# A kernel whose instruction order is written by its own estimate of times: the estimate learns a lock between two engines

## The chip, the cores and the metric

The kernel runs on one core of a Trainium2 chip. A core has TensorE (PE, matmuls into PSUM), VectorE (DVE), ScalarE (ACT), GpSimd (POOL) and SyncE (SP), which issues most of the transfers. Each engine works through its own list of instructions in order, and an instruction waits until the data that it reads are there. The metric is the time on the device in microseconds, the median of several runs.

## The reference

One inference step of a decoder layer on 1024 new prompt rows and 8 x 4 sample rows (1056 in all, width 1024, float32):

```
h = rmsnorm(x, norm_mix);  p = h @ w_in + b_in          # 1024 -> 4104
mLSTM heads (4): causal conv and silu on q, k; gates i, f; chunked scan with states C, n, m
HGRN2 heads (4): sigmoid gates f; chunked scan with state S
mix = concat(sigmoid(o) * headnorm(mLSTM), headnorm(HGRN2) * silu(g))
x = x + mix @ w_out
h2 = rmsnorm(x, norm_ffn)
x = x + (silu(h2 @ w_gate) * (h2 @ w_up)) @ w_down      # 1024 -> 2816 -> 1024
outputs: rmsnorm(x, norm_final) and the conv, C, n, m, S states of prompt and samples
```

## The kernel before, in words

Every dense product is made of three fast matmuls: an operand is rounded to a short format (the tiles HI for activations and whi for weights) and what the rounding left is kept beside it (LO and wlo); hi x hi, hi x lo and lo x hi are summed. ScalarE makes the rounded part and VectorE or GpSimd the rest, which the text calls the rest of a weight or of a row. `split(t, pool)` does this for weight tile t, 1024 columns in two chunks of 512 (L212 rounds, L213 makes the rest).

The 1056 rows lie in three blocks of 288, 384 and 384. The projection is a list of `units`, each one output tile of 128 columns for one block: 24 matmuls (L254, L256, L257; in the first unit of a block the low products come last, L265). For each of four mLSTM heads there are four weight tiles times three blocks, preceded by one tile for the gates (units 0, 6 and 11), and then the same for four HGRN2 heads. Unit 5 is block 1's first, unit 10 block 2's first. Then come the output projection `w_out` (units from `first_wo` on, by quarters of 264 rows), the second norm `norm2`, a few plain feed-forward tiles, and from some 700 us on the rest of the feed-forward in a scheme with fewer products, whose order is written out by step counts.

Everything beside the dense units is written as Python generators that emit instructions in pieces and are interleaved with the units: `startup(b)` (first norm of block b: sums of squares, a power on GpSimd, a transpose that spreads it over the partitions, then per row tile a scaling on VectorE L1940, a rounding on ScalarE L1943 and a rest L1947), `gates` and `gates_sample` (running sums and maxima for the mLSTM gates), `conv`, `mix_a` (mLSTM: L685 to L766), `mix_b` (HGRN2), `sample_core`, `split`, `mix_split` (rounds the mixers' output), `norm2`. Between matmuls `hook` steps them. A piece is emitted either after a count of hooks (`yield 2`) or when `need(e, ...)` says yes: the kernel keeps an estimate of each engine's time, of each tile's last write and read and of the transfers (`now`, `wrote`, `read`), advanced by `estimate()` with `cost()` for each instruction, and `need` asks whether the operands are there by that engine's time and whether that engine is at most 2.0 us ahead of TensorE. `finish(key)` forces a generator to its end where its result is needed next. So the numbers in `cost` decide the order of the instructions, and nothing else: the order is fixed when the program is built.

Weight tiles live in rings: two raw buffers, five whi and five wlo (`NRAW`, `NW`). In the kernel before, tiles 2 to 8 (`NAUTO = 9`) are rounded when `need("ACT", raw)` agrees, later ones by hook counts, and all the rests from tile 2 on are made by GpSimd. SP's list is in order: a load that waits for its buffer holds what is behind it.

Of the kernel before, what the change touches and what calls it, by code (L numbers as in the profile page):

```python
# [10 lines left out]
F32 = mybir.dt.float32  # L11
# [30 lines left out]
def hybrid_step(ctx: ExitStack, tc: tile.TileContext, i, o):  # L42
# [17 lines left out]

    now = dict(PE=0.0, DVE=0.0, ACT=0.0, POOL=0.0, SP=0.0, dma=0.0, n=0, tab="T", on=True)
    wrote, read, rings, pred, cap = {}, {}, {}, {}, {}
    ENG = {"PE": "PE", "DVE": "DVE", "Activation": "ACT", "Pool": "POOL", "SP": "SP"}

    def keys_of(ap):
# [17 lines left out]
    def all_keys(aps):  # L83
        return [k for a in aps if hasattr(a.tensor, "tag_meta") for k in keys_of(a)]

    def cost(e, op, x, n):
        if e == "PE":
            a = x.ins[0]
            if a.dtype == F32R:
                return 0.0076 + 0.000433 * n  # L90
            return 0.01 + n * (0.00078 if "transpose" in x.concise()[:400].lower() else 0.0017)
        if e == "DVE":
            return 0.13 + (0.0018 if "Scan" in op else 0.00104) * n
        if e == "ACT":
            c = 0.1 + 0.00083 * n
            f = str(getattr(x, "func", ""))
            for tab, fs in (("L", ("Ln",)), ("T", ("Tanh",)), ("S", ("Sigmoid", "Silu"))):
                if any(f.endswith(y) for y in fs) and now["tab"] != tab:
                    now["tab"] = tab
                    c += 1.28  # L100
            return c
        return 0.25 + 0.002 * n

    def estimate():
        if not now["on"]:
            return
        for x in islice(nc.all_instructions(), now["n"], None):
            now["n"] += 1
            e = ENG.get(str(x.engine).split(".")[-1])
            outs = [a.bass_ap for a in x.outs if hasattr(a, "bass_ap")]  # L110
            if e is None or not outs:
                continue
            ins = [a.bass_ap for a in x.ins if hasattr(a, "bass_ap")]
            op = str(x.opcode)
            n = 1
            for q in outs[0].ap[1:]:
                n *= q[1]
            ko, ki = all_keys(outs), all_keys(ins)
            t = max([now[e]] + [wrote.get(k, 0.0) + 0.06 for k in ki])
            for k in ko:  # L120
                if not (e == "PE" and k in wrote):
                    t = max(t, touched(k) + 0.06)
                if k not in wrote and pred[k[0]]:
                    t = max(t, read.get(pred[k[0]], 0.0) + 0.06)
            if "DMA" in op:
                now[e] = t + 0.4
                now["dma"] = max(now["dma"], t) + n * outs[0].ap[0][1] * 4 / 385e3
                end = now["dma"] + 1.8
            else:
                now[e] = t + cost(e, op, x, n)  # L130
# [8 lines left out]
    def need(e, *aps, banks=0, tags=(), lead=0.0):  # L139
        def ok():  # L140
            t = max([wrote.get(k, 0.0) for k in all_keys(aps)] + [0.0])
            for tag, m in (("mx", banks), *((x, 1) for x in tags)):
                for full in rings:
                    if m and full.startswith(tag + "_"):
                        r, b = rings[full], cap[full]
                        t = max([t] + [read.get(k, 0.0) for k in r[-b:][:m] if len(r) >= b])
            if e == "PE":
                return t <= now["PE"] + lead
            return t <= max(now["PE"], now[e]) + lead and now[e] <= now["PE"] + 2.0
        return ok  # L150

    def start(gen, key, wait=1):
        active.append([gen, key, wait])
# [34 lines left out]
                if callable(e[2]) and (e[1] == key or k > 8):  # L188
                    step_gen(e)

    NW, NRAW, NAUTO = 5, 2, 9
    raws, his, los = {}, {}, {}

    def load(t):
# [4 lines left out]
    def split(t, pool):  # L199
        while t not in raws or (t and t - 1 not in his):  # L200
            yield 1
        hi = his[t] = wp.tile([128, 1024], F32R, tag="whi", name="whi", bufs=NW)
        lo = los[t] = wp.tile([128, 1024], F32R, tag="wlo", name="wlo", bufs=NW)
        n, raw = tile_n[t], raws[t]
        auto = t >= 2 and t < NAUTO
        for c in range(0, n, 512):
            if auto:
                yield need("ACT", raw)
            elif c:
                yield 2  # L210
            s = slice(c, c + 512)
            nc.scalar.activation(hi[:, s], raw[:, s], AF.Copy)  # L212
            (nc.gpsimd if pool else nc.vector).tensor_tensor(lo[:, s], raw[:, s], hi[:, s].bitcast(F32), op=OP.subtract)  # L213
# [117 lines left out]
    nc.scalar.dma_start(vec, i["vec"])  # L331
    maskneg, seqm, mneg4 = cst[:, 0:128], cst[:, 128:136], cst[:, 136:168]
    mk = {0: msk[:, 80:112], **{l: msk[:, 16 * j:16 * j + 16] for j, l in enumerate(LEVELS)}}
    nc.scalar.preload_act_table_set("sqrt_and_others")
    ones = cn.tile([128, 1], F32, name="ones")
    nc.vector.memset(ones, 1.0)
    mhalf = cn.tile([128, 5], F32, name="mhalf")
# [2 lines left out]
    def col(j):  # L340
        return vec[:, j:j + 1]

    def ntile(tag="nt"):
        if tag in ("raw", "W"):
            return mp.tile([128, 387], F32, tag=tag, name=tag, bufs=2 if tag == "raw" else 1)
        if tag == "na":
            return cn.tile([128, QN], F32, tag=tag, name=tag, bufs=1)
        return cn.tile([128, 384], F32, tag=tag, name=tag, bufs=2)

    def norm_rstd(key, n, acc, w=(2, 3)):  # L350

# [89 lines left out]
    def gates(ps, b):  # L441
# [16 lines left out]
        nc.scalar.activation(a, f, AF.Abs)  # L458
        nc.scalar.activation(a, a, AF.Exp, scale=-1.0)
        nc.scalar.activation(a, a, AF.Ln, bias=1.0)  # L460
        yield need("DVE", a)
        nc.vector.scalar_tensor_tensor(lf, f, 0.0, a, op0=OP.min, op1=OP.subtract)
        nc.vector.tensor_copy(me[:, 0:1], mcar)
# [40 lines left out]
    def gates_sample(ig, lf):  # L504
# [19 lines left out]
        g, em, wl, ng, wi = (r[:, j] for j in range(5))  # L524
        nc.vector.tensor_tensor(g, s4(ig), F4, op=OP.subtract)
        nc.vector.tensor_tensor(ng, F4, m4, op=OP.subtract)
        nc.scalar.activation(em, m4, AF.Exp, scale=-2.0)
        nc.vector.tensor_tensor(wi, ng, m0s[:, :, None].to_broadcast([4, 8, 4]), op=OP.add)
        nc.scalar.activation(wi, wi, AF.Exp)
        nc.vector.tensor_tensor(wl, g, ng[:, :, 3:4].to_broadcast([4, 8, 4]), op=OP.add)  # L530
# [657 lines left out]
    def mix_split(th):  # L1188
        hv, lv = half(HI, th), half(LO, th)
        n = 528 if th == 0 else 496  # L1190
        for m in range(KT):
            while any(("a" if m < 4 else "b", m % 4, b) not in done for b in range(2 + th)):
                yield 2
# [6 lines left out]
            yield 1  # L1200
        if th:
            while ("sb",) not in done:
                yield 1
# [6 lines left out]
    def out_evac(m, q):  # L1210
        def ev(ps):
            x = xq(q)
            nc.vector.tensor_tensor(x(m), x(m), ps[:, :QN], op=OP.add)
            dst = ntile(("raw", "raw", "W", "na")[q]) if m == 0 else ntile()
            nc.scalar.activation(dst[:, :QN], x(m), AF.Square)
            if m == 0:
                naccs[q] = dst
# [700 lines left out]
        nc.gpsimd.tensor_tensor(rs[:, 0:3], rs[:, 0:3], mhalf[:, 0:3], op=OP.pow)  # L1918

    def spread_nat(b, rs):  # L1920
        pb = bank()
        for t, c in parts_of(b):
            nc.tensor.transpose(pb[:, 128 * t:128 * t + c], rs[:c, t:t + 1].to_broadcast([c, 128]), ident[:c, :c])
        return pb

    def startup(b):
        for t in range(3):
            x = xn[b, t]
            yield need("ACT" if b == 2 else "DVE", *(x if isinstance(x, tuple) else (x,)))
            rs = squares_nat(b, rs if t else None, (t,))  # L1930
        yield need("DVE", rs)
        rstd_nat(rs)
        yield need("PE", rs, banks=1)
        pb = spread_nat(b, rs)
        x, hv, lv = xb(b), hb(HI, b), hb(LO, b)
        for j in range(KT + 2):
# [279 lines left out]
```

## Time and profile before

| | |
|---|---|
| median of 3 runs | 1365.42 us (1364.0 to 1366.39) |
| profiled execution | 1364.32 us, span 1362.3 us |
| TensorE busy | 1326.3 us (97%) |
| VectorE, ScalarE, GpSimd busy | 875.2, 555.3, 593.3 us |
| mean granted TensorE clock | 0.987 |

In rows of the profile an instruction is named by its line, engine, operation and tiles (out<-in). A row of waits says which instruction waited for which, how long in total, how often and the longest time. A row of stretches has the length, then for PE, PEld (weight load), DVE, ACT and POOL the busy time and the number of instructions, and last the granted TensorE clock, the share of the transfer engines and GB/s. A row in order of time has start, duration, engine, line and operation, how many were merged (x3), and in brackets the idle time before and who ended it.

### The profile page before, as it was taken

To read this page: it belongs to the slowest core of one execution; us is meant where nothing else is said; L and a number is where in the kernel's file an instruction comes from. 1 tells how busy PE (TensorE), PEld (TensorE's weight loads), DVE (VectorE), ACT (ScalarE), POOL (GpSimd) and SP (SyncE) were. 2 spreads that over 40 slices of the span, in tenths; PEclk is the share of its full clock that TensorE was granted. 3 is DMA by queue.
4 is the path that set the end of the run, shared out by engine and by line. 5 is a ranking of instruction groups with operands and counts; after the bars stand their busy time and mean duration, and the time that the engine had idled before them with its cause. 6 is when DMAs were issued, how large, how long until landed. Compare 5 with 4: busy or idle time off the path is not lost.

```text
span 1362.3 us, 29321 instructions
## 1 busy us (share of the span) xinstructions
PE 1326.3 (97%) x11584; PEld 1293.9 (95%) x11584; DVE 875.2 (64%) x2051; ACT 555.3 (41%) x1309; POOL 593.3 (44%) x561
## 2 busy tenths in 40 slices
PE   7989999999999999999999999999999999999996
PEld 6889999999999997999999999999999999999995
DVE  7867657664655557734875676676664347777765
ACT  6653434234434434323445444455444342212232
POOL 4322213232221323123566656565666585444434
PEclk8999999999999999999999999999999999999997
DMA  9012202331111114533306666755764289878733
GB/s 356 26 56 69 68 28 87 106 95 33 44 33 40 47 36 148 177 102 112 107 27 229 222 237 210 253 207 213 246 214 151 69 295 352 289 283 293 268 147 128
DMA packets 104961, 207.79 MB, mean 153 GB/s; under 512 B 10944, under 2 KB 59992, under 8 KB 104312
## 3 DMA queue, kind: packets, MB, share of 16 engines
q1 hardware_dynamic: 104392, 205.65, 43.4%
q8 instruction: 91, 1.49, 0.4%
q14 instruction: 46, 0.38, 0.1%
q10 hardware_dynamic: 432, 0.27, 0.1%
HBM read 143.76 MB, written 62.13 MB: 151 GB/s over the span
## 4 chain that ended last, share of the span: by engine, by line
PE 87%; DVE 8%; ACT 2%; issue 2%; POOL 1%; DMA 1%; POOLq 0%; DVEq 0%; ACTq 0%
PE mx L1488 17%; PE mm L254 11%; PE mm L257 10%; PE mm L256 10%; PE mm L1488 10%; PE mx L1711 8%; PE mm L1711 5%; PE so L1488 3%; PE mx L971 1%; PE mx L823 1%; PE so L1711 1%; PE mx L1752 1%; PE mm L1752 1%; DVE ck L593 1%; PE mx L1093 1%
## 5 line engine op out<-in xcount | busy, mean ns | idle before, releaser
L254 PE MATMUL mm<-HI,whi 128*128 128x384 f32 (+2 forms) x1160 | 379.1, 327 | 3.7 <-ACT HI L1943 2.0
L257 PE MATMUL mm<-HI,wlo 128*128 128x384 f32 (+2 forms) x1160 | 363.3, 313 | 2.7 <-DVE wlo L213 1.9
L256 PE MATMUL mm<-LO,whi 128*128 128x384 f32 (+2 forms) x1136 | 352.7, 310 | 0.0
L254 PEld LDWEIGHTS mm<-HI,whi 128*128 128x128 f32 x1160 | 220.9, 190 | 9.5 <-ACT HI L1943 3.5
L257 PEld LDWEIGHTS mm<-HI,wlo 128*128 128x128 f32 x1160 | 220.6, 190 | 3.4 <-DVE wlo L213 2.4
L256 PEld LDWEIGHTS mm<-LO,whi 128*128 128x128 f32 x1136 | 215.0, 189 | 0.0
L213 POOL TENSOR_TENSOR wlo<-raw,whi 128x512 fp32r<-128x512 f32 x86 | 114.4, 1339 | 202.6 <-ACT whi L212 202.5
L1417 POOL TENSOR_TENSOR wlo<-S,whi 128x512 fp32r<-128x512 f32 x78 | 110.8, 1426 | 90.0 <-ACT whi L1416 87.0
L1488 PE MATMUL mx<-T,whi 128*128 128x264 f32 x640 | 118.7, 285 | 0.0
L1488 PEld LDWEIGHTS mx<-T,whi 128*128 128x128 f32 x640 | 99.2, 188 | 0.0
L1541 POOL TENSOR_TENSOR LO<-rg,HI 128x528 fp32r<-128x528 f32 x52 | 70.8, 1370 | 64.2 <-ACT HI L1540 64.2
L1488 PE MATMUL mx<-HI,whi 128*128 128x264 f32 x320 | 91.2, 285 | 0.0
L1488 PE MATMUL mx<-T,wlo 128*128 128x264 f32 x320 | 91.0, 284 | 0.0
L1488 PE MATMUL mx<-LO,whi 128*128 128x264 f32 x320 | 90.9, 284 | 0.0
L1488 PE MATMUL mx<-HI,wlo 128*128 128x264 f32 x320 | 90.8, 284 | 0.0
L1629 DVE TENSOR_TENSOR fh<-fr,fh 128x512 fp32r<-128x512 f32 x80 | 67.9, 849 | 32.0 <-ACT fh L1624 31.7
L1715 DVE TENSOR_TENSOR X<-X,mx 128x264 f32<-128x264 f32 x160 | 65.4, 424 | 25.0 <-PE mx L1711 24.3
L1416 ACT ACTIVATE whi<-S 128x512 fp32r<-128x512 f32 x80 | 50.3, 630 | 72.7 <-DVE S L1405 68.8
L1540 ACT ACTIVATE HI<-rg 128x528 fp32r<-128x528 f32 x52 | 32.3, 641 | 104.0 <-PE mx L1711 31.9
L1488 PE MATMUL mm<-HI,wlo 128*128 128x264 f32 x240 | 68.3, 285 | 0.0
L1488 PE MATMUL mm<-HI,whi 128*128 128x264 f32 x240 | 68.1, 284 | 0.0
L1488 PE MATMUL mm<-LO,whi 128*128 128x264 f32 x240 | 67.7, 282 | 0.0
(549 smaller groups left out, 3422.8 us busy)
## 6 DMA issues: line engine op xcount, KB each, us to landing
d_wf<-fh SPq DMA_DIRECT2D x60, 512.0 KB
rg<-d_ff SPq DMA_DIRECT2D x42, 528.0 KB
raw<-in_wA SPq DMA_DIRECT2D x31, 512.0 KB
whi<-d_wf SPq DMA_DIRECT2D x29, 512.0 KB
wlo<-d_wf SPq DMA_DIRECT2D x28, 512.0 KB
raw<-in_wgu SPq DMA_DIRECT2D x24, 512.0 KB
d_ff<-sg SPq DMA_DIRECT2D x40, 264.0 KB
rg<-in_wgu SPq DMA_DIRECT2D x20, 512.0 KB
```

What stands on the lines that cost most here:

```text
L213: (nc.gpsimd if pool else nc.vector).tensor_tensor(lo[:, s], raw[:, s], hi[:, s].bitcast(F32), op=OP.subtract)
L254: nc.tensor.matmul(ps[:, :n], wh, rh[:, kk, :], start=(k == 0), stop=False)
L256: nc.tensor.matmul(ps[:, :n], wh, rl[:, kk, :], start=False, stop=False)
L257: nc.tensor.matmul(ps[:, :n], wl, rh[:, kk, :], start=False, stop=(k == nk - 1 and not late))
L1416: nc.scalar.activation(hi[:, s], t, AF.Copy)
L1417: (nc.vector if dve else nc.gpsimd).tensor_tensor(lo[:, s], t, hi[:, s].bitcast(F32), op=OP.subtract)
L1488: nc.tensor.matmul(ps[:, :QN], a[:, w], b_[kk][:, c], start=new and kk == 0 and x == 0, stop=kk == 3 and x == 2, skip_group_check=True)
L1540: nc.scalar.activation(h, src, AF.Copy)
L1541: (nc.vector if dve else nc.gpsimd).tensor_tensor(lw, src, h.bitcast(F32), op=OP.subtract)
L1629: nc.vector.tensor_tensor(lw, src, h.bitcast(F32), op=OP.subtract)
L1711: nc.tensor.matmul(ps[:, :QN], a[:, w], b_[k][:, cs], start=new and k == 0 and x == 0, stop=k == 1 and x == 2, skip_group_check=True)
L1715: nc.vector.tensor_tensor(y, y, ps[:, :QN], op=OP.add)
```

## The change

- `cost` gets other numbers (VectorE 0.08 us fixed instead of 0.13, powers on GpSimd 0.85 us, small matmuls, memsets, TensorE's costs doubled below 15 us, activation tables).
- A new function `shared` says whether an instruction uses what VectorE and GpSimd share, and `estimate` lets one of them start behind the other's hold.
- `need` takes a margin of 0.3 us for TensorE and a parameter `ahead`.
- `NAUTO` goes from 9 to 99: every later weight tile is split under `need`, and from tile 5 on the rest goes to VectorE, or to GpSimd where VectorE's estimated time is over 0.5 us ahead of TensorE's and GpSimd's is less.
- First steps: block 2's norm starts only when block 1's is done, its spread uses the bank `so`; the gates' transposes are asked for with a lead of -1.0; the sample gates start behind block 1's gates; the table for exp is loaded first and again behind the log.
- `mix_split` waits by `need` instead of by counts; the running sums of the second norm use other buffers.

```diff
+    held = {"DVE": [], "POOL": []}
...
         if e == "DVE":
-            return 0.13 + (0.0018 if "Scan" in op else 0.00104) * n
+            return 0.08 + (0.0018 if "Scan" in op else 0.00104) * n
...
-        return 0.25 + 0.002 * n
+        if "Memset" in op:
+            return 0.1 + 0.0008 * n
+        return 0.85 if n < 8 and "TensorTensor" in op else 0.24 + 0.002 * n
+
+    def shared(e, op, ins, outs):
+
+        sb = [a for a in ins if a.tensor.name[:3] not in ("mx_", "mm_", "so_")]
+        if e == "POOL":
+            return 2 if sb else 1
+        big = [a for a in sb if wide(a)]
+        if len(big) > 1:
+            return 1
+        return 2 if len(ins) == len(sb) and big and ("Copy" in op or "TensorScalar" in op) else 0
...
+                d = cost(e, op, x, n, outs)
+                if e in held:
+                    mine = shared(e, op, ins, outs)
+                    for s, f, m in held["POOL" if e == "DVE" else "DVE"][-8:]:
+                        if mine and m + mine > 2 and s <= t < f:
+                            t = f
+                    if mine:
+                        held[e].append((t, t + d, mine))
+                now[e] = t + d
...
             if e == "PE":
-                return t <= now["PE"] + lead
-            return t <= max(now["PE"], now[e]) + lead and now[e] <= now["PE"] + 2.0
+                return t <= now["PE"] + lead - 0.3
+            return t <= max(now["PE"], now[e]) + lead and now[e] <= now["PE"] + ahead
...
-    NW, NRAW, NAUTO = 5, 2, 9
+    NW, NRAW, NAUTO = 5, 2, 99
...
-                yield need("ACT", raw)
+                yield need("ACT", raw, ahead=2.0 if t > 4 else 4.0)
...
             nc.scalar.activation(hi[:, s], raw[:, s], AF.Copy)
+            if auto and t > 4:
+                yield need("DVE", hi[:, s])
+                pool = now["DVE"] > now["PE"] + 0.5 and now["POOL"] < now["DVE"]
             (nc.gpsimd if pool else nc.vector).tensor_tensor(lo[:, s], raw[:, s], hi[:, s].bitcast(F32), op=OP.subtract)
...
-    nc.scalar.preload_act_table_set("sqrt_and_others")
+    nc.scalar.preload_act_table_set("exp_and_others")
...
         nc.scalar.activation(a, a, AF.Ln, bias=1.0)
+        nc.scalar.preload_act_table_set("exp_and_others")
...
-        yield need("PE", wi, wl, em, banks=2)
+        yield need("PE", wi, wl, em, banks=2, lead=-1.0)
...
-            start(gates_sample(ig, lf), ("gsm",), 40)
+            start(gates_sample(ig, lf), ("gsm",))
...
+        while ("g", 1) not in done:
+            yield need("DVE")
...
-                yield 2
+                yield need("PE")
             src = xr(m, 528 * th, 528 * th + n)
+            yield need("ACT", src, ahead=0.0 if th else 2.0)
             nc.scalar.activation(hv[:, m, 0:n], src, AF.Copy)
+            yield need("DVE", hv[:, m, 0:n], ahead=0.0 if th else 2.0)
...
-            dst = ntile(("raw", "raw", "W", "na")[q]) if m == 0 else ntile()
+            dst = tl(("cq", "v", "ngb", "ngb")[q], 384, q // 2 + 1) if m == 0 else ntile()
...
-        pb = bank()
+        pb = bank("so" if b else "mx")
...
     def startup(b):
+        while b == 2 and ("n1", 1) not in done:
+            yield need("ACT")
...
-        yield need("PE", rs, banks=1)
+        yield need("PE", rs, tags=("so",))
```

More of the change, by code (lines that the diff above doesn't have):

```diff
@@ L84, in all_keys, with wide, cost @@
         return [k for a in aps if hasattr(a.tensor, "tag_meta") for k in keys_of(a)]
-    def cost(e, op, x, n):
+    def wide(ap):
+        return any(q[1] > 1 for q in ap.ap[1:])
+    def cost(e, op, x, n, outs):
         if e == "PE":
[L88 to L91, printed above, removed]
+            if x.ins[0].dtype == F32R:
+                c = 0.0076 + 0.000433 * n
+            elif "transpose" in x.concise()[:400].lower():
+                c = 0.01 + n * 0.00078
+            else:
+                c = 0.004 + n * (0.00174 if outs[0].ap[0][1] > 32 else 0.00044)
+            return c * (2 if now["PE"] < 15 else 1)
         if e == "DVE":
-            return 0.13 + (0.0018 if "Scan" in op else 0.00104) * n
+            return 0.08 + (0.0018 if "Scan" in op else 0.00104) * n
         if e == "ACT":
@@ L96, in cost @@
             f = str(getattr(x, "func", ""))
-            for tab, fs in (("L", ("Ln",)), ("T", ("Tanh",)), ("S", ("Sigmoid", "Silu"))):
+            for tab, fs in (("L", ("Ln",)), ("T", ("Tanh", "Exp")), ("S", ("Sigmoid",)), ("U", ("Silu",))):
                 if any(f.endswith(y) for y in fs) and now["tab"] != tab:
@@ L110, in estimate @@
             outs = [a.bass_ap for a in x.outs if hasattr(a, "bass_ap")]
+            if e == "ACT" and "LoadAct" in str(x.opcode) and now["tab"] != "T":
+                now["tab"] = "T"
+                now["ACT"] += 1.28
             if e is None or not outs:
@@ L126, in estimate @@
                 now[e] = t + 0.4
-                now["dma"] = max(now["dma"], t) + n * outs[0].ap[0][1] * 4 / 385e3
-                end = now["dma"] + 1.8
-            else:
-                now[e] = t + cost(e, op, x, n)
+                now["dma"] = max(now["dma"], t) + n * outs[0].ap[0][1] * 4 / 350e3
+                end = now["dma"] + 2.0
+            else:
+                d = cost(e, op, x, n, outs)
[7 more added lines that the diff above has]
+                now[e] = t + d
                 end = now[e] + (0.1 if e != "PE" else 0.06)
@@ L137, in estimate, with need @@
                 read[k[0]] = max(read.get(k[0], 0.0), end if k in ko or "DMA" in op else now[e])
-    def need(e, *aps, banks=0, tags=(), lead=0.0):
+    def need(e, *aps, banks=0, tags=(), lead=0.0, ahead=2.0):
         def ok():
@@ L341, in col, with ntile @@
         return vec[:, j:j + 1]
[L343 to L348, printed above, removed]
+    def ntile():
+        return cn.tile([128, 384], F32, tag="nt", name="nt", bufs=2)
     def norm_rstd(key, n, acc, w=(2, 3)):
@@ L526, in gates_sample @@
         nc.vector.tensor_tensor(ng, F4, m4, op=OP.subtract)
+        nc.vector.tensor_tensor(wi, ng, m0s[:, :, None].to_broadcast([4, 8, 4]), op=OP.add)
+        nc.vector.tensor_tensor(wl, g, ng[:, :, 3:4].to_broadcast([4, 8, 4]), op=OP.add)
+        yield need("ACT", r)
         nc.scalar.activation(em, m4, AF.Exp, scale=-2.0)
-        nc.vector.tensor_tensor(wi, ng, m0s[:, :, None].to_broadcast([4, 8, 4]), op=OP.add)
         nc.scalar.activation(wi, wi, AF.Exp)
-        nc.vector.tensor_tensor(wl, g, ng[:, :, 3:4].to_broadcast([4, 8, 4]), op=OP.add)
         nc.scalar.activation(wl, wl, AF.Exp)
-        yield 2
         mo = mp.tile([4, 8], F32, tag="mso", name="mso")
@@ L1192, in mix_split @@
             while any(("a" if m < 4 else "b", m % 4, b) not in done for b in range(2 + th)):
-                yield 2
+                yield need("PE")
             src = xr(m, 528 * th, 528 * th + n)
+            yield need("ACT", src, ahead=0.0 if th else 2.0)
             nc.scalar.activation(hv[:, m, 0:n], src, AF.Copy)
+            yield need("DVE", hv[:, m, 0:n], ahead=0.0 if th else 2.0)
             nc.vector.tensor_tensor(lv[:, m, 0:n], src, hv[:, m, 0:n].bitcast(F32), op=OP.subtract)
@@ L1199, in mix_split @@
             done.add(("split", th, m))
-            yield 1
         if th:
             while ("sb",) not in done:
-                yield 1
+                yield need("PE")
+            yield need("ACT", smx)
             nc.scalar.activation(hv[:, :, 496:528], smx, AF.Copy)
```

## The prediction

> **What bounds the kernel now.** I read the page's busy shares and slices first, then busy time by stage, then the list of what TensorE waited for, and only then the time order of single engines around those waits. The profiled execution took 1364.32 us (span 1362.3 and 2.0 around it), 1.10 us under the median 1365.42. All terms are made against 1364.32 and the 1.10 is put back at the end.
>
> ```profile
> span 1362.3 us, 29321 instructions
> PE 1326.3 (97%) x11584; PEld 1293.9 (95%) x11584; DVE 875.2 (64%) x2051; ACT 555.3 (41%) x1309; POOL 593.3 (44%) x561
> ...
> 0.00:200.00 200.00, 183.97 (x1148) 177.58 (x1149) 141.74 (x368) 101.44 (x237) 62.07 (x78) 0.95 0.30 103
> 200.00:400.00 200.00, 196.60 (x2002) 186.00 (x2001) 121.62 (x400) 76.44 (x219) 54.58 (x85) 1.00 0.21 64
> 400.00:560.00 160.00, 156.48 (x2030) 145.00 (x2029) 102.60 (x331) 71.39 (x211) 46.41 (x57) 1.00 0.26 82
> ...
> 300.00:350.00 50.00, 50.00 (x665) 47.09 (x664) 27.00 (x100) 21.13 (x64) 14.34 (x14) 1.00 0.12 37
> ```
>
> TensorE sets the end: it is busy 97% of the span. The rules that the diff edits are consulted in the mixer stage and up to the second norm, about the first 700 us; behind that the order is written out by hook counts that the diff leaves alone. The stage rows hold columns PE, PEld, DVE, ACT, POOL, clock, DMA. TensorE is idle 16.0 + 3.4 + 3.5 = 22.9 us in the first 560 us (200 - 183.97, and so on), and slowed at a clock of 0.95 in the first. No rearrangement can earn more than that idle time and that clock, some 30 us; what it can reasonably earn are the waits in the next list.
>
> ```profile
> PE mx L1923 <- POOL nrs L1918: 3.0, 2, 2.5
> PE mx L743 <- DVE C L730: 2.5, 1, 2.5
> PE mx L702 <- DVE kt L712: 2.1, 1, 2.1
> PE so L852 <- DMA st<-in_S: 2.1, 2, 1.3
> PE mm L254 <- ACT HI L1943: 2.0, 1, 2.0
> PE mm L257 <- DVE wlo L213: 1.9, 2, 1.0
> PE mx L720 <- DVE kt L712: 1.2, 1, 1.2
> PE mx L494 <- ACT AT L482: 1.0, 1, 1.0
> PE mx L874 <- DVE sjunk L871: 1.0, 1, 1.0
> PE mx L1093 <- DVE kt L1084: 0.9, 1, 0.9
> PE mm L257 <- POOL wlo L213: 0.8, 1, 0.8
> ...
> PE mx L1236 <- DVE nrs L1232: 0.6, 1, 0.6
> ```
>
> Each row is a matmul placed into TensorE's stream before its operand was there (total, times, longest). TensorE has other matmuls to run meanwhile, so a wait here is a wrong guess of the emission, worth its whole length. Of L1923's 3.0 us, 2.5 are in the first 10 us, which nothing edited touches, and 0.5 belong to block 2's norm.
>
> **Part 1: the lock and the durations in the estimate.** Why the guesses were wrong is seen where the same VectorE instructions run with and without GpSimd beside them.
>
> ```profile
> 64.65 1.03 DVE L467 TENSOR_TENSOR_SCAN gC<-ones,gB 4x128 f32<-4x128 f32 x3
> 90.25 4.04 DVE L467 TENSOR_TENSOR_SCAN gC<-ones,gB 4x128 f32<-4x128 f32 x3
> ...
> 90.03 3.99 POOL L213 TENSOR_TENSOR wlo<-raw,whi 128x512 fp32r<-128x512 f32 x3 [3.08 <-ACT whi L212]
> ...
> 62.05 1.92 DVE L593 SCALAR_TENSOR_TENSOR ck<-raw,vec,ck 128x384 f32<-128x384 f32 x3
> ...
> 143.86 3.83 DVE L593 SCALAR_TENSOR_TENSOR qB<-raw,vec,qB 128x384 f32<-128x384 f32 x3 [0.39 <-ACT qB L571]
> ...
> L670 POOL TENSOR_TENSOR sm<-sm,mhalf 128x3 f32<-128x3 f32 x16 | 14.2, 889 | 59.8 <-DVE sm L668 35.6 <-DVE sm L665 16.1 <-DVE raw L583 8.0
> ```
>
> Three scans take 1.03 us alone and 4.04 us beside three weight rests on GpSimd; three conv steps take 1.92 or 3.83 us. The old formula gives the scans 3 x (0.13 + 0.0018 x 128) = 1.08 us in both cases, so VectorE's clock in the estimate was 3.0 us early at 94 us, and the matmul L743 was placed 2.5 us too soon behind it. The new estimate moves a VectorE start behind a GpSimd hold and would see it. The power on 128x3 takes 889 ns; the old estimate gave 0.25 + 0.002 x 3 = 0.26 us, the new one 0.85. TensorE's insertions also get a margin of 0.3 us. No instruction is added by all this; its cost is that a chain of mixer steps runs later, 0.3 us for each step on TensorE, covered by the dense matmuls of the other units (400 to 560 us: 156.48 of 160 busy).
>
> The stall at L743 has a second price, as has the one around 31 to 33 us:
>
> ```profile
> 34.00:37.00 3.00, 3.00 (x14) 3.00 (x14) 2.90 (x16) 0.44 (x1) 0.00 (x0) 0.52 0.08 30
> ...
> 95.00:98.00 3.00, 0.49 (x5) 0.29 (x3) 2.81 (x7) 0.93 (x2) 0.00 (x0) 1.00 0.48 177
> 98.00:107.00 9.00, 8.97 (x50) 8.73 (x51) 8.79 (x19) 5.09 (x17) 5.36 (x4) 0.62 0.35 109
> ...
> 236.00:240.00 4.00, 3.27 (x20) 3.31 (x21) 2.18 (x7) 2.11 (x5) 1.82 (x8) 1.00 0.00 0
> ```
>
> Behind the pause at 95 to 98 us the clock is 0.62 for 9 us: 9 x 0.38 = 3.4 us lost. Behind the 2.1 us pause of L702 near 236 us it stays 1.00. So a pause of this size sometimes costs the clock. I take 2.5 + 3.4 = 5.9 us for L743 (between 0 and 5.9). [...]
>
> The rest of the list that comes from guesses, L702 2.1, L720 1.2, L874 1.0, L1093 0.9, L1236 0.6, sums to 5.8 us. I take three quarters, 4.3 (bounds 0 and 5.8). L852's 2.1 us wait for transfers into two buffers; their order is not edited: 0. L1923 for block 2 gives 0.5.
>
> Against it: three conv steps take 1.92 us, 0.64 each; the old formula gives 0.53 for 384 columns and the new one 0.48. Uncontended VectorE blocks are thus guessed shorter than before, by 0.16 us against 0.11 on each step, which the 0.3 us margin covers for two steps and not for a block of ten. From this I let new waits return a third of what is earned.
>
> **Part 2: weight rests.** A rest of 128x512 is 1.3 us on GpSimd and 0.69 us at best on VectorE.
>
> ```profile
> L213 POOL TENSOR_TENSOR wlo<-raw,whi 128x512 fp32r<-128x512 f32 x82 | 108.4, 1331 | 202.6 <-ACT whi L212 202.5
> ...
> L213 DVE TENSOR_TENSOR wlo<-raw,whi x4: 686/1224/1762, 9.5 to 18.5; 128x512 fp32r<-128x512 f32 x4
> ```
>
> From tile 5 on, both the rounding on ScalarE and the rest wait for the estimate's word, and the rest goes to VectorE unless that is over 0.5 us ahead of TensorE and GpSimd is less far. If all of the 82 went over, VectorE would have at most 82 x 0.69 = 57 us more, beside 141.7 + 121.6 + 102.6 = 366 of 560 us so far, and its scans and convs would lose the delays shown above. This lies under TensorE's matmuls; I count 0 for the work and 0.4 for the 0.8 us wait at a late rest (bounds: 0.8 gained; the loss is the third rival's).
>
> **Part 3: first steps.** Block 2's sums of squares now wait until block 1's norm is done.
>
> ```profile
> 36.47 2.18 DVE L1940 SCALAR_TENSOR_TENSOR X<-X,vec,mx 128x384 f32<-128x384 f32 x4
> ...
> 38.01 1.05 ACT L1913 ACTIVATE raw<-raw 128x1024 f32<-128x1024 f32 x1
> ...
> 39.05 1.76 ACT L1943 ACTIVATE HI<-X 128x384 fp32r<-128x384 f32 x4
> ...
> 39.62 0.46 PE L254 MATMUL mm<-HI,whi 128*128 128x384 f32 x1 [2.04 <-ACT HI L1943]
> ...
> 30.71 8.80 SPq L223 DMA_DIRECT2D raw<-in_wA  x2
> 39.60 0.28 SPq L484 DMA_DIRECT2D d_bc<-C  x1
> ```
>
> The first scaled row is ready at 36.47 + 2.18/4 = 37.0, but ScalarE squares block 2's row from 38.01 before it rounds at 39.05, and TensorE starts unit 5 at 39.62 after 2.04 us of waiting. Without the square the rounding can start at 38.01, or at 37.0 if it is emitted ahead of the bias of the unit just finished: a gain of 1.04 to 2.04; I take 1.5. The gate transposes with lead -1.0 take away the 1.0 us of L494 and perhaps the clock of 0.52 behind it (3 x 0.48 = 1.4), but TensorE then only reaches unit 5 earlier and waits for the same rounding: 0, and 2.4 at most if the scaling, too, is emitted ahead of the convs.
>
> What is moved: the square frees the buffer into which the sixth weight tile is loaded, and that load held SP's queue until 39.6 us. With the square behind block 1's norm it is held until eight rows are scaled, rounded and rested: with 0.55 us of VectorE for a scaling and, as an estimate, as much for each rest that it takes, to some 44 us, 5 us or more longer, and the gate rows' stores and the loads that bring them back to all partitions stand behind it. The first mixer chain thus begins that much later. Its cover is block 1's and 2's dense units; without it, 5 us. Count 0. The squares' own lateness is covered as well: block 2's first unit has its eight low products, the last that it needs, at 68.7 to 69.9:
>
> ```profile
> L265 PE MATMUL mm<-LO,whi x8: 334/334/334, 68.7 to 69.9; 128*128 128x384 f32 x8
> ```
>
>
> The activation table: one load of exp goes away in front of the first gate's chain and one is moved ahead.
>
> ```profile
> 19.01 1.28 ACT L459 ACT_TABLE_LOAD   x1
> ...
> 23.09 1.22 DVE L1911 SCALAR_TENSOR_TENSOR xn<-xn 128x1024 f32<-128x1024 f32 x1
> 24.35 1.42 DVE L462 SCALAR_TENSOR_TENSOR AT<-AT,AT 4x288 f32<-4x288 f32 x1
> ```
>
> It takes 1.28 us, and the gate's next step L462 waits for VectorE's squares anyway, until 24.35: 0.
>
> The mixer's split that waits by need instead of counts, the sample gates behind block 1's gates, the other bank for the norm's spread and the other buffers for the sums add no instruction; they stand beside dense matmuls: 0 each, within the third that returns.
>
> **Sum.** 5.9 + 4.3 + 0.5 + 0.4 + 1.5 = 12.6 us earned. A third returns, 4.2, which leaves 8.4: 1364.3 - 8.4 = 1355.9, and with the 1.1 to the median 1357.0.
>
> **Rivals.** First, a **larger gain**: no new waits, the scaling ahead of the convs and all of the guesses mended: 5.9 + 5.8 + 0.5 + 0.8 + 2.0 + 2.4 = 17.4, so 1348. For it speaks that from 300 to 350 us TensorE is busy in all of the 50 us, even by the old guesses; against it the shorter VectorE formula. Second, **the waits only move**: mending the guess at one place pushes the block to the next, all 12.6 us come back, 1365. That is also the case in which the estimate's locks don't follow the chip's. Third, **late weight rests**, the one that ends slower: under the old rule tiles from 9 on were split at fixed counts and TensorE never waited for one of them; of the four tiles 5 to 8 under the estimate's rule one was 0.8 us late. With about 36 tiles more under it and a ring of five buffers, a tile whose rest is put off until the deadline of its unit makes TensorE wait 0.8 us. From 8.4/0.8 = 11 late tiles on nothing is gained; at 22 it is 17.6 - 8.4 = 9 us slower, 1375. Against it: a tile's split may start about four units before its first use. Fourth, **the clock does not come back**: the slow stretch at 98 us has another cause and stays. Then 12.6 - 3.4 = 9.2, a third returns, 6.1 remain: 1359.3. [...]
>
> **Chances.** Forecast 0.46, larger gain 0.17, waits only move 0.15, late rests 0.13, clock stays 0.09. About 0.2% (2.7 us) is what a measurement of this kernel tells from no change. Faster: the forecast, the larger gain and the clock case make 0.72. Of the second rival 0.12 is same and 0.03 slower; late rests make 0.12 slower and 0.01 same: 0.13 same, 0.15 slower. The forecast's own range is 1351 to 1362; with the larger gain's 1348 and the second rival's 1365 and their spread the range is 1346 to 1367, which leaves out the late rests and tails, about 0.2.
>
> **What would show it.** Right: L743, L702, L720 and L874 gone from TensorE's waits or under 0.5 us each, the clock at 1.00 from 95 to 110 us, unit 5 starting before 38.6 us, weight rests on VectorE in the groups, and the stretch behind 700 us as long as before. Wrong: a row of L257 waiting for wlo with ten or more times (late rests); new rows of the same total (waits move); unit 10 waiting for block 2's roundings (the moved squares were not covered).

## The result, and the profile after

The changed kernel takes 1350.33 us (median of 4, 1348.47 to 1353.72), the kernel before 1364.71 us (median of 4). The ratio is 0.9896, interval 0.9873 to 0.9918: faster by 1.0%, 14.4 us between the medians. The forecast was 1357; the time lies 0.7 us below the forecast's own range of 1351 to 1362, inside the full range, and next to the rival "larger gain" (1348).

The page of the changed kernel and its stages, in the columns used before:

```profile
span 1348.7 us, 29340 instructions
PE 1318.8 (98%) x11584; PEld 1287.9 (95%) x11584; DVE 887.3 (66%) x2102; ACT 554.1 (41%) x1308; POOL 531.3 (39%) x510
...
0.00:200.00 200.00, 186.23 (x1208) 180.07 (x1208) 150.15 (x387) 104.31 (x245) 58.33 (x75) 0.99 0.32 107
200.00:400.00 200.00, 198.31 (x2104) 187.63 (x2104) 126.73 (x434) 76.73 (x226) 30.13 (x65) 1.00 0.22 67
400.00:560.00 160.00, 158.15 (x1974) 147.68 (x1973) 103.00 (x337) 67.92 (x204) 30.18 (x43) 0.99 0.25 78
560.00:700.00 140.00, 140.00 (x1150) 139.06 (x1149) 88.78 (x185) 52.24 (x114) 46.04 (x40) 1.00 0.31 100
```

TensorE is idle 13.77 + 1.69 + 1.85 = 17.3 us in the first 560 us, where it was 22.9: 5.6 us less. But units 0 to 4 start within 0.2 us of before (unit 4 at 29.6 us), so what differs in the first 31 us earns nothing. Behind it the first stage reads, before and after:

```profile
31.00:200.00 169.00, 159.91 (x1012) 155.31 (x1012) 118.73 (x325) 80.57 (x200) 46.75 (x61) 0.96 0.18 57
```

```profile
31.00:200.00 169.00, 163.76 (x1072) 159.71 (x1072) 127.07 (x343) 83.87 (x207) 43.63 (x59) 1.00 0.20 62
```

From 31 to 700 us the idle time falls from 9.1 + 3.4 + 3.5 + 0.6 = 16.6 to 5.2 + 1.7 + 1.9 + 0 = 8.8 us, 7.8 less. The clock gives some 169 x 0.04 = 6.8 us, of which the stretch at 400 to 560 us loses 160 x 0.01 = 1.6 again. Together that is 13.0 of the 13.7 us that the changed kernel gains in its profile behind unit 4: three fifths idle time, two fifths clock. In its clock the profiled pair flatters the change: over the executions on record the mean granted clock is 0.988 before (38 executions) and 0.990 in the four of the changed kernel, an estimated 0.002 x 1350 = 2.7 us, where the two profiled ones have 0.987 and 0.991. The waits of TensorE between 17 and 700 us:

```profile
PE mm L290 <- DVE wlo L246: 2.7, 3, 1.0
PE mx L752 <- DVE kt L744: 2.3, 1, 2.3
PE mx L906 <- DVE sjunk L903: 1.8, 1, 1.8
PE mx L727 <- DVE ck L632: 1.2, 1, 1.2
PE mm L287 <- ACT HI L1979: 0.9, 3, 0.4
PE mx L290 <- POOL wlo L246: 0.8, 1, 0.8
PE mx L752 <- ACT kB L665: 0.7, 1, 0.7
PE so L884 <- DMA st<-in_C: 0.5, 1, 0.5
```

(L752 was L720 before, L906 was L874, L727 was L695, L290 was L257, L1979 was L1943.) The old rows of L743, L702, L1093 and L1236 are gone. New or longer ones stand in their place: L752 2.3, L906 1.8, L727 1.2. The waits were partly removed and partly exchanged.

Because both kernels run the same dense matmuls in the same order, the start of the n-th can be compared. The table counts them in units of 24 and shows how many microseconds earlier than in the profile of before each profiled kernel starts a unit (the first row has the times of before). Mixer work placed earlier or later between the units shifts single entries by some microseconds, and each row is one execution, while those of the changed kernel lie up to 5 us apart (1348.47 to 1353.72).

```
unit                 5    10    30    60    95   110   150  last
before, start us  39.6  65.9 171.0 330.5 513.8 588.3 712.2 1337.1
changed            4.4   7.0  10.2  11.9  12.7  12.8  13.9  14.0
first steps only   2.2   2.0   6.9   5.9   6.0   5.7   5.8   5.8
estimate only      2.8   4.7  11.6  11.8  13.3   2.6   3.7   2.3
estimate+buffers   3.7   5.6  12.4  12.7  14.0   8.1   9.2   7.8
tiles to 9 only    4.7   7.3   9.8   9.8  11.1  15.3  15.5  11.6
no lock            2.3   1.9   6.2   8.5   9.2  12.4  10.4  10.4
old buffers        3.8   6.4   7.4   9.7  10.6   8.5   9.7   9.7
block 2 early      3.7   6.4   9.5  11.3  12.4  12.5  13.6  12.5
VectorE 0.13       3.6   5.0   6.2   5.0   5.2   6.9  -5.9  -6.0
0.13, 3.0 ahead    4.0   6.8   2.4   0.2   0.3   0.9  -7.5  -7.5
before with 0.08   2.0   0.1   3.6  -1.9  -3.0  -4.2  -8.1  -8.1
no margin          4.6   7.4   3.2   4.1   0.7   4.9   6.0   4.9
VectorE 0.06       3.7   6.5  10.7  12.4  13.6  16.7  17.8  16.6
```

Half of the gain (7.0 us) is there at unit 10, 10 us at unit 30, and in the changed kernel nothing changes behind unit 150, where the order is written out by counts (in some of the others it does: with tiles to 9, 3.9 us are lost there).

### The profile page after: what moved, and what is told of

It reads as the page before. It is cut to its first block, busy times and chain, and to the rows that moved or that the text cites. A ratio compares the mean times of both kernels' runs of the same rounds, so it can differ in the third digit from the quotient of the medians.

```text
span 1348.7 us, 29340 instructions
## 1 busy us (share of the span) xinstructions
PE 1318.8 (98%) x11584; PEld 1287.9 (95%) x11584; DVE 887.3 (66%) x2102; ACT 554.1 (41%) x1308; POOL 531.3 (39%) x510
## 4 chain that ended last, share of the span: by engine, by line
PE 91%; DVE 5%; ACT 1%; DMA 1%; issue 1%; POOL 0%; SPq 0%; POOLq 0%; ACTq 0%; DVEq 0%
PE mx L1522 17%; PE mm L287 12%; PE mm L290 12%; PE mm L289 11%; PE mm L1522 10%; PE mx L1745 8%; PE mm L1745 5%; PE so L1522 3%; PE mx L1003 1%; PE so L1745 1%; PE mx L855 1%; PE mx L1786 1%; PE mm L1786 1%; PE mx L752 1%; PE mx L1145 1%
## 5 line engine op out<-in xcount | busy, mean ns | idle before, releaser
L290 PE MATMUL mm<-HI,wlo 128*128 128x384 f32 (+2 forms) x1160 | 362.0, 312 | 2.7 <-DVE wlo L246 2.7
L290 PEld LDWEIGHTS mm<-HI,wlo 128*128 128x128 f32 x1160 | 219.5, 189 | 3.5 <-DVE wlo L246 3.5
L1451 POOL TENSOR_TENSOR wlo<-S,whi 128x512 fp32r<-128x512 f32 x78 | 110.8, 1426 | 91.7 <-ACT whi L1450 88.6
L702 POOL TENSOR_TENSOR sm<-sm,mhalf 128x3 f32<-128x3 f32 (+2 forms) x26 | 21.4, 821 | 147.0 <-DVE sm L700 75.3
L246 POOL TENSOR_TENSOR wlo<-raw,whi 128x512 fp32r<-128x512 f32 x35 | 48.8, 1403 | 60.0 <-ACT whi L242 58.1
```

The costliest lines, as they stand in the source:

```text
L290: nc.tensor.matmul(ps[:, :n], wl, rh[:, kk, :], start=False, stop=(k == nk - 1 and not late))
L1451: (nc.vector if dve else nc.gpsimd).tensor_tensor(lo[:, s], t, hi[:, s].bitcast(F32), op=OP.subtract)
```

## The experiments

Ratios are to the kernel before, of several rounds on the same chip; the changed kernel's is 0.9896.

**First steps alone, and the estimate alone.** The first edit puts into the kernel before the two table loads, the lead of -1.0, the sample gates' start, the bank `so` and block 2's gate; the second only `cost`, `shared`, `held`, the margin and the estimate of the transfers.

> The kernel before with the first steps alone (tables, lead -1.0, sample gates behind block 1's gates, spread into the bank so, block 2's norm behind block 1's); estimate and weight rests as before. Theory A, the first steps earn on their own: unit 5 starts 4 us earlier (near 35.3 us instead of 39.6), unit 10 about 7 us earlier, and of these 7 us at least 5 are left at the end: 1357 to 1360, ratio 0.994 to 0.996. Rival B, the first steps earn only because the estimate orders them: with the old estimate unit 5 starts at 37.6 or later and the end is 1362 to 1365, ratio over 0.998.

> The kernel before with the estimate alone (costs, lock, margin of 0.3 us). Theory A: the later waits of TensorE (L743, L702, L720, L874 and their like) lose half of their length, the first 60 us stay within 1 us of before: 1358 to 1361, ratio 0.994 to 0.997. Rival B: the estimate brings nearly all, 1352 to 1355, ratio under 0.993, with unit 5 at 37 us or earlier. Rival C: the estimate alone only moves the waits: 1364, ratio 0.998 to 1.002.

First steps alone: 1359.23 us, ratio 0.9963 (0.9946 to 0.9980). Theory A's range at the end, but unit 5 gains 2.2 instead of 4, unit 10 only 2.0 instead of 7. The estimate alone: 1362.34 us, 0.9992 (0.9982 to 1.0003). Rival C by the total, and yet the table says otherwise: it is 13.3 us ahead at unit 95, more than the changed kernel, and 2.6 us at unit 110. The mixers' order is as good as the changed kernel's, and all of it is lost where the output projection starts. In the estimate-only kernel's time order of single engines and in its stretches:

```profile
541.12 0.99 PE L1161 MATMUL mx<-ident,kt 128*128 128x128 f32 x3 [3.61 <-DVE kt L1156]
...
553.82 0.42 ACT L1245 ACTIVATE raw<-X 128x264 f32<-128x264 f32 x1 [6.36 <-PE mx L1103]
...
541.00:547.00 6.00, 4.34 (x60) 3.48 (x61) 5.15 (x22) 2.16 (x7) 0.00 (x0) 0.50 0.64 197
550.00:557.00 7.00, 4.05 (x41) 3.75 (x36) 2.41 (x10) 1.43 (x5) 0.00 (x0) 0.95 0.00 0
```

Two things stop it. TensorE waits 3.6 us at L1161, and its clock is 0.50 from 541 to 547 us. Then ScalarE's square L1245 of an output unit writes into a buffer `raw` that the last HGRN2 head's v still holds, so it stands 6.4 us until the transposes L1103 have read it, with the evacuations of the output projection behind it; TensorE is idle 2.95 us of the 7 us from 550 us on.

**The buffers.** The edit, into the estimate-only kernel, and the reverse out of the changed one:

```diff
-            dst = ntile(("raw", "raw", "W", "na")[q]) if m == 0 else ntile()
+            dst = tl(("cq", "v", "ngb", "ngb")[q], 384, q // 2 + 1) if m == 0 else ntile()
```

> The kernel before with the new estimate and with the other buffers for the running sums of the second norm (the sums of quarters 0 and 1 no longer in the two buffers that the last HGRN2 head's q and v hold); first steps, weight rests and the mixer's split as before. Theory A, the estimate earns some 13 us in the mixers and loses them where the output projection starts, because its evacuations wait for those two buffers: unit 110 now stays 12 us or more ahead, 1349 to 1353, ratio 0.989 to 0.992. Rival B, the loss at the hand-over comes from the mixer's split by hook counts: unit 110 falls back to 3 us ahead as without the edit, 1361 to 1363, ratio 0.998 to 1.0.

> The changed kernel with the old buffers for the running sums. Theory A: units 95 to 110 lose 8 us or more, with ScalarE's squares waiting for the last mixer's transposes: 1358 to 1363, ratio 0.995 to 0.999. Rival B: nothing, since the mixer's split by need has brought the last head's chain forward: 1349 to 1351, ratio 0.989 to 0.991.

The estimate with the buffers: 1358.04, 0.9963 (0.9950 to 0.9976), 4.3 us better than without; unit 110 is 8.1 ahead, not 12. The changed kernel with the old buffers: 1353.6, 0.9933 (0.9918 to 0.9948), 3.3 us worse. Its row loses 2.2 us between units 10 and 30, in the slow clock behind one pause (0.55 for 6 us, last section), with which the buffers have nothing to do, and 2.1 between units 95 and 110 that the changed kernel doesn't lose. The waits of ScalarE from 500 to 600 us show the same stall there, and hardly any of it in the kernel before:

```profile
ACT raw L1253 <- PE mx L1109: 3.4, 1, 3.4
```

```profile
ACT raw L1215 <- PE mx L1073: 0.6, 1, 0.6
```

So theory A holds in kind, at half its size in the estimate-only kernel and at a quarter in the changed one. What the estimate with the buffers still loses there (14.0 to 8.1, with a wait of 3.8 us at L1161 and the slow clock behind it, 0.50 from 540.6 to 546.6 us) comes from what else differs. The weight tiles from 9 on are not needed for it, since the row with tiles to 9 loses nothing there; the mixer's split was not tried by itself, so this stays open.

**Weight tiles put back to hook counts from tile 9 on** (`NAUTO` 99 to 9):

> The changed kernel with the bound for tiles under the estimate put back from 99 to 9, so that weight tiles from 9 on are split by hook counts and their rests are made by GpSimd. Theory A, weight rests on VectorE are worth nothing by themselves since no matmul waits for them: ratio 0.989 to 0.992, as the changed kernel. Rival B, they take GpSimd's holds away from VectorE's chains: VectorE's scans and convs get longer again and 3 us or more are lost: ratio 0.992 to 0.996.

1351.1 us, 0.9904 (0.9885 to 0.9923): theory A, no difference from the changed kernel at the end. Its profiled execution, the slowest of its four, is 2.5 us ahead of the changed kernel's at unit 110 and loses 3.9 behind unit 150. In the changed kernel 55 of the rests run on VectorE at half of GpSimd's time,

```profile
L246 DVE TENSOR_TENSOR wlo<-raw,whi x55: 675/685/1761, 9.4 to 1088.9; 128x512 fp32r<-128x512 f32 x55
L246 POOL TENSOR_TENSOR wlo<-raw,whi x35: 1272/1297/1920, 27.5 to 1089.6; 128x512 fp32r<-128x512 f32 x35
```

and TensorE hardly notices: its waits for rests (L290) all lie in the first 200 us, and no tile behind that was late.

**The estimate without the lock** (the condition in `estimate` made false):

```diff
-                        if mine and m + mine > 2 and s <= t < f:
+                        if False:
```

> The changed kernel whose estimate never lets one of the two engines wait for the other's hold; all costs and all else stay. Theory A, the lock in the estimate earns about half of what lies behind the first 60 us: 3 us lost, ratio 0.991 to 0.994, with TensorE's waits for VectorE (kt, C, ck) growing by 3 us. Rival B, the lock is not what matters (costs and margin are): within 1 us of the changed kernel, ratio 0.989 to 0.990. Rival C: the kernel's order is so sensitive that any edit of the estimate moves the end by 2 us either way.

1357.44 us, 0.9945 (0.9924 to 0.9966): 0.0049 more than the changed kernel's ratio, which is 6.7 us, twice theory A's number. Its profiled execution is the fastest of the four (1353.9), and by the table it is 5.1 us behind the changed kernel at unit 10, 0.4 at unit 110 and 3.5 at the end. The loss in front shows in a matmul of unit 4, without the lock and with it:

```profile
33.02 0.40 PE L290 MATMUL mx<-HI,wlo 128*128 128x288 f32 x1 [2.86 <-POOL wlo L246]
```

```profile
31.53 0.40 PE L290 MATMUL mx<-HI,wlo 128*128 128x288 f32 x1 [0.82 <-POOL wlo L246]
```

Without the lock GpSimd gets the norm's power ahead of this rest, and block 1's scaling starts at 36.06 us instead of 34.04. So part of what the lock earns lies in the first 60 us, not behind it, where theory A put all of it. Rival C, that any edit of the estimate moves the end, is not excluded: other edits of one number below move it by 3.5 to 20 us.

**Block 2's norm not behind block 1's:**

```diff
-        while b == 2 and ("n1", 1) not in done:
-            yield need("ACT")
```

> The changed kernel whose block 2 norm does not wait for block 1's. Theory A, this gate is what clears ScalarE at unit 5: unit 5 starts 1 to 2 us later (36.3 to 37.3 us) and 1 to 3 us are lost at unit 10; at the end 1351 to 1353. Rival B, with the new estimate the squares fall elsewhere anyway: unit 5 within 0.5 us of 35.3, end within 1 us of the changed kernel.

1351.51 us, 0.9919 (0.9902 to 0.9935); unit 5 is 0.7 us later than in the changed kernel, unit 10 0.6. Neither theory hits both numbers: unit 5 is nearer to rival B, the end lies in theory A's range. The mechanism is rival B's: with the gate gone the squares are still emitted behind the roundings, as its ScalarE shows:

```profile
39.56 1.05 ACT L1977 ACTIVATE HI<-X 128x384 fp32r<-128x384 f32 x2 [0.47 <-DVE X L1974]
40.52 1.05 ACT L1947 ACTIVATE raw<-raw 128x1024 f32<-128x1024 f32 x1
```

**One number of the estimate.** VectorE's fixed cost in the changed kernel back from 0.08 to 0.13, the same with more room ahead of TensorE (3.0 us instead of 2.0), 0.08 in the kernel before, and 0.06 in the changed kernel:

```diff
-            return 0.08 + (0.0018 if "Scan" in op else 0.00104) * n
+            return 0.13 + (0.0018 if "Scan" in op else 0.00104) * n
```

> The changed kernel with VectorE's fixed cost back at 0.13 us. Theory A, the smaller number guesses blocks of VectorE too short (three conv steps take 1.92 us, 1.44 by it and 1.59 by the old one), so going back mends waits behind long VectorE blocks: TensorE's waits between 60 and 560 us (6.0 us in the changed kernel) fall by 2 us or more, 1347 to 1349. Rival B, the margin of 0.3 us covers it: 1349 to 1352. Rival C, small instructions (0.08 us apart in the trace) matter more and going back costs 2 us or more: 1352 to 1355.

> The changed kernel with VectorE's fixed cost back at 0.13 us (which alone gave 1370) and with the bound on how far an engine may be ahead of TensorE at 3.0 us instead of 2.0 where no other is given. Theory A, a larger cost hurts because it reaches that bound sooner and holds pieces back, above all the preparation of the feed-forward's operands: with the bound at 3.0 the 12.5 us of waits at 700 to 715 us (6.2, 3.2, 2.1 and the half clock) go and the end is 1349 to 1357. Rival B, it hurts because the order of pieces among themselves changes with each duration: the bound doesn't mend it, 1362 to 1372.

> The kernel before with one number changed: VectorE's fixed cost in the estimate 0.08 us instead of 0.13. Putting 0.13 back into the changed kernel cost 20 us, 5 to 6 of them in the mixers and 14 where the feed-forward's operands are prepared. Theory A, the number works by letting pieces for VectorE out earlier (an engine may be at most 2 us ahead of TensorE), whatever the rest of the estimate: the mixers get 3 us or more faster, 1358 to 1361, ratio 0.995 to 0.998. Rival B, the number only suits the changed kernel's other costs, and the old estimate was tuned around 0.13: 1363 to 1370, ratio 1.0 to 1.005.

> The changed kernel with VectorE's fixed cost at 0.06 us. Theory A, smaller is better still (pieces leave earlier): 1346 to 1349, ratio under 0.989. Rival B, 0.08 lies at an edge found by trying and a step of 0.02 loses: 1352 to 1360, with one or two new waits of TensorE of over 2 us that name the place. If the step loses, the gain of the change is in part a chosen number and not a better model.

0.13: 1370.35 us, 1.0056 (1.0037 to 1.0074), 20 us worse than the changed kernel and slower than before. Rival C, far beyond its number. Some 6 us go in the mixers; 6.9 + 5.9 = 12.8 more between units 110 and 150, where the feed-forward's operands are prepared (waits at 560 to 760 us):

```profile
PE mm L1522 <- ACT T L1398: 6.2, 1, 6.2
PE mm L1522 <- POOL T L1399: 3.2, 1, 3.2
PE mm L1522 <- ACT nt L1530: 2.1, 1, 2.1
```

With the bound at 3.0: 1370.77, 1.0054 (1.0037 to 1.0071). The same place costs 0.9 + 7.5 = 8.4 us instead of 12.8, but the mixers lose 11.9 instead of 5.9 by unit 110. Its VectorE row `706.84 0.83 DVE L1392` is the last of that preparation and stands behind seven weight sums and rests (L1439, L1451); in the changed kernel it starts at 685.12, behind four. So a wider bound does not mend it: theory A falls, rival B holds, and the order of the pieces among each other does differ. Why it tips there at 0.13 was not followed further. 0.08 in the kernel before: 1371.48, 1.0061 (1.0043 to 1.0080), 7.6 us worse; rival B again, a little beyond its range. 0.06: 1346.86 us, 0.9870 (0.9854 to 0.9887), 3.5 us under the changed kernel's median; theory A. Its runs (1346.01 to 1347.97) all lie under the changed kernel's (1348.47 to 1353.72), though the two intervals of the ratio overlap. It is the fastest of all that were run; its idle TensorE time in 400 to 560 us is 0.3 us:

```profile
400.00:560.00 160.00, 159.67 (x1960) 149.45 (x1957) 105.64 (x345) 68.59 (x207) 29.09 (x43) 1.00 0.26 81
```

**No margin** (`lead - 0.3` back to `lead`):

> The changed kernel without the margin of 0.3 us that TensorE's insertions must wait. Theory A, the margin covers the durations guessed too short: without it the waits of TensorE in the mixers grow by a third of a microsecond at some ten places, 2 to 4 us lost, ratio 0.991 to 0.993. Rival B, an insertion 0.3 us earlier starts its chain earlier, and the two cancel: within 1 us of the changed kernel. Rival C: the order tips at one hand-over and 5 us or more go either way.

1359.82 us, 0.9968 (0.9956 to 0.9980): 9.5 us lost. Rival C by size; the waits of its mixers (60 to 700 us) are of the kind that theory A names, few and long:

```profile
PE mx L793 <- DVE kt L788: 3.3, 2, 3.1
PE mx L727 <- DVE ck L632: 2.9, 2, 1.6
PE mm L287 <- ACT whi L242: 2.2, 1, 2.2
PE mx L1089 <- DVE wib L1030: 2.1, 3, 0.7
```

## Why the prediction was right or wrong

**What bounds the kernel** was right: the whole gain lies in front of unit 150, in TensorE's idle time and clock, and the stretch behind it takes as long as before. Of the signs named, L743 and L702 are gone, the clock is 1.00 from 95 to 110 us, unit 5 starts at 35.3 us and unit 10 waits for no rounding of block 2; but L720 (now L752) and L874 (now L906) still wait.

**First steps: 1.5 us for the rounding and 0.5 for block 2's power, measured 7.0 at unit 10.** The step that failed is the 0 for the case put at "2.4 at most if the scaling, too, is emitted ahead of the convs". The rounding itself came as said, at the upper end of 1.04 to 2.04: with the first steps alone the scaling starts at 36.23, nearly where it was, but the square is out of the way, the rounding follows at once, and unit 5 gains 2.2 us:

```profile
36.88 2.10 ACT L1948 ACTIVATE HI<-X 128x384 fp32r<-128x384 f32 x4 [0.30 <-DVE X L1945]
```

What moves the scaling is the estimate: with the estimate alone it starts at 34.37, while the squares still hold the rounding until 36.27:

```profile
34.37 2.18 DVE L1970 SCALAR_TENSOR_TENSOR X<-X,vec,mx 128x384 f32<-128x384 f32 x4
...
36.27 0.51 ACT L1973 ACTIVATE HI<-X 128x384 fp32r<-128x384 f32 x1
```

The changed kernel has both, as its VectorE and ScalarE show:

```profile
34.04 1.13 DVE L1976 SCALAR_TENSOR_TENSOR X<-X,vec,so 128x384 f32<-128x384 f32 x2
...
34.68 1.05 ACT L1979 ACTIVATE HI<-X 128x384 fp32r<-128x384 f32 x2 [2.48 <-DVE X L1976]
```

The scaling starts at 34.04 instead of 36.47, ahead of the k conv; the roundings at 34.68 instead of 39.05: 2.4 + 2.0 = 4.4 us at unit 5. Block 2's gate is not what clears the square away there, as the run without it shows; which of the first steps does stays open. The gates' wait is gone as said, and with it the slow clock at 33.5 to 36.9 us (0.50), which the prediction saw (1.4 us) and dropped because TensorE "only reaches unit 5 earlier". It overlooked a second slow stretch, at 40.3 to 43.7 us (0.50), behind the wait for the rounding. The stretch 31 to 45 us, before and after:

```profile
31.00:45.00 14.00, 10.61 (x46) 8.73 (x46) 12.24 (x37) 8.28 (x17) 5.87 (x6) 0.76 0.42 141
```

```profile
31.00:45.00 14.00, 12.47 (x70) 10.29 (x71) 13.05 (x43) 9.42 (x24) 7.04 (x9) 1.00 0.37 126
```

The clock alone is 14 x 0.24 = 3.4 us here, and half of it lies behind the start of unit 5. That these are first steps is only partly so: first steps alone gain 2.0 at unit 10, the estimate alone 4.7, both with the rest 7.0.

**L743 with its clock: 5.9 us, of which 3.2 came (units 10 to 30).** Its wait of 2.5 us and the 0.8 of the late rest went; a wait of 2.3 at L752 and 0.8 at a rest came in the same stretch. The gates' block is on VectorE again, beside GpSimd's rests (a step of 4x384 takes 1.5 us there, and 0.55 once they are done), and the matmul was placed too soon in spite of the lock; why the new estimate missed it is not shown. GpSimd, VectorE and TensorE there:

```profile
81.35 5.02 POOL L246 TENSOR_TENSOR wlo<-raw,whi 128x512 fp32r<-128x512 f32 x3 [1.61 <-ACT whi L242]
...
83.71 1.52 DVE L506 TENSOR_TENSOR gC<-gC,gm 4x384 f32<-4x384 f32 x1
85.27 1.51 DVE L508 TENSOR_TENSOR gB<-gC,gm 4x384 f32<-4x384 f32 x1
86.82 0.55 DVE L509 TENSOR_TENSOR gA<-gA,gC 4x384 f32<-4x384 f32 x1
...
88.01 0.94 PE L752 MATMUL mx<-vt,kt 128*128 128x129 f32 x6 [2.29 <-DVE kt L744]
```

Only the 3.4 us of clock came back, and that is luck: in two other kernels with the same wait the clock fell to 0.55 and 0.56 (last section).

**The other guesses: 4.3 us.** L702, L1093 and L1236 went, and L720 at its old place (1.2 us, between 130 and 165 us): 4.8 of the 5.8 us listed. L874 grew from 1.0 to 1.8, and L852's wait for transfers, counted at 0, fell from 2.1 to 0.5. In TensorE's idle time of 200 to 700 us it is 7.5 before (3.40 + 3.52 + 0.55) and 3.5 after (1.69 + 1.85 + 0): 3.9 us, with the new waits of that stretch already taken off. About right.

**A third returns: 4.2 us.** New at L752 are 2.3 + 0.7 us, L906 grew by 0.8 and L727 (0.3 before) by 0.9: 4.7 us; the late rest of 0.8 only changed its place. About right.

**Weight rests: 0 for the work** was right (0.9904 against 0.9896), and the rival "late rests" did not come. **The other buffers, 0**, missed a dependence: they are worth 4.3 us in the estimate-only kernel and up to 3.3 in the changed one (2.1 by the table). The step "they stand beside dense matmuls" looked at what the buffers add and not at who holds them: the last head's v in `raw`, behind which ScalarE stood 6.4 us. In the trace of before, where it stood 0.6 us, this could hardly be read; it shows in the new order.

**The moved square and SP's queue.** The sixth weight tile's load held SP's queue longer, as said, by less: the gate rows' store is at 41.45 instead of 39.60, 1.9 us and not 5, since block 1's norm itself came earlier.

```profile
31.50 9.86 SPq L256 DMA_DIRECT2D raw<-in_wA  x2
41.45 0.28 SPq L514 DMA_DIRECT2D d_bc<-C  x1
```

**VectorE's shorter formula, "against it"**, pointed the wrong way: the larger number, nearer to the long instructions, costs 20 us. The prediction read the estimate as a model whose errors turn into waits one by one. The runs show parts that add up only in places: at unit 10 the first steps and the estimate nearly do, but by the medians the first steps alone give 4 us, the estimate alone 1 and the buffers 4 on top of it, together 9 of the 14; the mixer's split has no run of its own. And 0.08 for 0.13 is worth 20 us in one setting and costs 7.6 in the other.

**Where the sum fell short.** With a third taken off every term, it has 1.3 us in front of unit 10 and 7.1 behind it; the table has 7.0 and 6.9. So nearly all of what is missing (6 us by the medians) lies in the first steps: above all the early scaling and the clock behind unit 5. That the part behind fits so well is partly luck, with the clock behind L752 and the buffers in it.

## What to carry to other kernels

Where the order of instructions is worked out from estimated times, a changed number is a new order: measure it whole, and look for the place where a good order is given back, by comparing the starts of the same work units in both traces. The estimate alone looked worthless (0.9992) and was 13 us ahead until the hand-over to the next stage, where one buffer, still held by the last piece of the stage before, stopped an evacuation and cost some 4 us of it. And when a stall is mended, ask what clock ran behind it before counting on it.

## What the runs showed of the hardware

Behind one and the same pause of TensorE the clock was 0.55 and 0.56 in two kernels and 1.00 in two others. Four kernels here have the wait of L752 with 2.28 to 2.31 us in the same surroundings; the 6 us behind it, in the kernel with tiles to 9, the changed one, the one with block 2 early and the one with the old buffers:

```profile
87.67:93.67 6.00, 6.00 (x33) 5.70 (x34) 4.16 (x13) 1.43 (x4) 0.00 (x0) 0.56 0.40 139
```

```profile
88.01:94.01 6.00, 6.00 (x52) 5.82 (x53) 5.26 (x19) 2.74 (x9) 0.00 (x0) 1.00 0.43 143
```

```profile
88.62:94.62 6.00, 6.00 (x52) 5.82 (x53) 5.27 (x19) 2.73 (x9) 0.00 (x0) 1.00 0.53 134
```

```profile
88.59:94.59 6.00, 6.00 (x32) 5.70 (x33) 4.16 (x13) 1.32 (x4) 0.00 (x0) 0.55 0.42 144
```

Twice 1.00, twice 0.55 or 0.56, which is 6 x 0.45 = 2.7 us for the same pause. In the profile of before, the slow stretches between 30 and 110 us are multiples of 3.41 us: they run from 33.47 to 36.88, from 40.30 to 43.71 and from 98.32 to 105.15 us, each at 0.50, so they last 3.41, 3.41 and 6.83 us, and their starts lie 6.83 and 58.02 us apart, 2 and 17 times 3.413. I call 3.413 us a step, an estimate from these numbers, and count the steps of the changed kernel back from its slow stretch at 533.36 to 536.78 us (0.50). With tiles to 9 the whole pause (85.39 to 87.67) lies in one stretch of this length, and the clock falls at the end of it. In the changed kernel (85.72 to 88.01) a step ends within the pause by this count (the next one ends at 89.63, 443.73 us or 130 steps ahead of 533.36), so that 1.79 us of idle time lie in one step, and the clock stays. The kernel with tiles to 9, then the changed one:

```profile
85.00:88.42 3.42, 1.14 (x10) 0.90 (x9) 3.36 (x6) 1.57 (x3) 1.03 (x1) 1.00 0.48 176
88.42:95.24 6.82, 6.82 (x36) 6.52 (x35) 4.37 (x18) 2.06 (x5) 0.00 (x0) 0.50 0.25 80
```

```profile
86.22:89.63 3.41, 1.62 (x13) 1.62 (x14) 3.31 (x9) 1.57 (x3) 0.15 (x1) 1.00 0.51 162
89.63:93.04 3.41, 3.41 (x33) 3.23 (x33) 2.74 (x9) 1.75 (x5) 0.00 (x0) 1.00 0.37 107
```

Idle time within a step is not all that decides it. In the profile of before, steps with 2.54 (94.91 to 98.32), 2.04 (36.88 to 40.30) and 1.56 us (30.06 to 33.47) of it were followed by 0.50, and one with 1.87 us (234.86 to 238.27) by 1.00; in the changed kernel one with 1.75 us (529.95 to 533.36) was followed by 0.50, and the one above with 1.79 us by 1.00. In these two kernels the 2.7 us go with how the pause lies to the steps, since its length was the same in both (2.28 and 2.29 us); more is not shown. The steps also speak against the rival "the clock does not come back": in the profile of before the pause of 2.5 us at L743 lies in one step, and the slow stretch begins at its end:

```profile
94.91:98.32 3.41, 0.87 (x8) 0.68 (x7) 3.21 (x8) 1.23 (x3) 0.00 (x0) 1.00 0.43 156
98.32:105.15 6.83, 6.83 (x36) 6.58 (x36) 6.62 (x14) 4.80 (x16) 4.74 (x4) 0.50 0.29 90
```
